# Merging two pairs of small matmul groups in a single-core diffusion step, with the instruction order set anew

## The chip, the core and the metric

The kernel runs on one core of a Trainium2 chip. The metric is device time in microseconds (us) of one execution. The core has a matmul engine (PE, with its weight loads shown apart as PEld), a vector engine (DVE), a scalar engine (ACT), a general engine (POOL) and a queue engine (SP) that only issues DMAs. Each engine runs its own instructions strictly in the order in which the program holds them, and waits at an instruction until what it needs is there.

## The reference

The reference computes one layer for 1024 latent tokens and 128 context tokens, with d_model 1024. Two token mixers read the same normalised, modulated input, through one projection:

```
u = h @ w_in                                   # 1024 -> 2560 (HGRN2) + 1760 (RWKV-7)
# HGRN2, 4 heads x 128, forward and backward, f = lb + (1 - lb) * sigmoid(z):
S = exp(b_last) * S + (k * exp(b_last - b))^T v ;  o = q * exp(b) S + (causal scores) v
# RWKV-7, 8 heads x 64, forward and backward, per token:
S = S * w - (S kk) (kk * a)^T + v k^T ;  y = S r
x = x + gate1 * (concat(o_a, o_b) @ w_out)
h = rmsnorm(x) * (1 + scale2) + shift2
x = x + gate2 * ((gelu(dwconv(h @ w_gate) + b) * (h @ w_up)) @ w_down)   # d_ff 2816
```

The outputs are the normalised tokens and the states that the context leaves in both mixers.

## The kernel before, in words

The whole step is recorded by a planner (class `Plan`) and then issued engine by engine. A recorded operation is one instruction, or a group made by `plan.together()`, which stands on its engine without anything between. The planner takes, for each engine in turn, the ready operation of the highest rank. The rank is the estimated rest of the path behind it, plus a lead by kind (`LEADS`) and a correction for each sixteen operations (`NUDGE`), less penalties for PE when the array's shape changes (`INTO`, `OUT`, `SWITCH`). Copies can go to ACT or DVE, and stores to POOL or SP, whichever the planner finds first. The order that results is fixed in the program.

Four stages follow one another, with overlap. They are named here by the lines of the profile.

- **Projections and RWKV features, about 60 to 500 us.** Lines L1125 to L1127 are the dense fp32r matmuls of the projection, three for each 128 rows of the contraction (high times high, low times high, high times low). Between them stand small fp32 groups of the RWKV features: `features(p, ...)` runs for 4 pairs of heads, over 3 blocks of 384 tokens each. In each block and each direction d it builds `kr` (L1452) and `kb` (L1453) on DVE, multiplies them chunk by chunk on PE in tiles of 64 x 32 (L1461 and L1462, 24 matmuls to a group, each run as two passes) into the PSUM tile `pk`, and copies the result out (L1469, L1475, L1477). `pk` has one buffer of two banks. `elim` (L1526, L1528) solves the small triangular systems.
- **Scans, about 500 to 1050 us.** `chains` is the sequential RWKV scan, 18 steps for each of two groups of heads (L1776, L1790, L1820, L1827, L1835, L1846). `hgrn_block(h, tb)` runs 12 times: it builds the HGRN2 scores in levels. Level 0 (L1631, 24 matmuls, tiles of 128 x 32) takes `kx` and `q2`; levels 1 to 5 (L1646) take `xs`, a copy of `kx` with the directions interleaved (L1643), and `qy` (L1618), which DVE updates between levels; `copy_predicated` (L1647) puts each level's part into `s32`. Then come L1652, L1658 and the transposes L1686 and L1691. The rest of the projection fills PE between these steps, and later the output projection (L2011 to L2013) with the row tiles' second norm and modulation (L2019, transposes L2025, L1991).
- **FFN up, about 1050 to 1535 us.** L2120, dense, with DVE's depthwise convolution (L2209) beside it. Its second half of tokens needs the quarter sums (L2057, L2053) of the row tiles that come last.
- **FFN down, to the end.** L2269 to L2271, dense. `finish` closes a row tile (L2290 to L2297), and `finish_last` the last one in pieces of 512, 256 and 256 columns (L2307 to L2323).

## Time and profile before

| what | us |
|---|---|
| median of 3 runs | 1820.85 (1820.06 to 1825.13) |
| the profiled execution | 1820.69 |
| its span, first to last instruction | 1818.9 |
| PE busy | 1768.3 (97%) |
| PE weight loads busy | 1587.1 (87%) |
| DVE busy | 1415.1 (78%) |
| ACT busy | 862.0 (47%) |

The granted TensorE clock was 0.993 over the span. Matmuls overlap in the pipeline and their ends are modelled, so a busy PE isn't one at its peak; what a matmul costs is read from the distance between the starts of neighbours.

### The profile page before, as it was taken

The numbers are of one execution on the slowest core, as the hardware profiler recorded it, in microseconds if no ns is written. First come the engines' busy times: TensorE is split into PE (matmuls) and PEld (weight loads), VectorE is DVE, ScalarE is ACT, GpSimd is POOL, SyncE is SP. The second block draws the span as 40 slices with busy tenths as digits, with TensorE's granted clock in tenths as the row PEclk, the third lists the DMA queues.
The fourth block names the chain that finished last, engine by engine and source line by source line (L and its number), as shares of the span: only waits on it lengthen the run. The fifth ranks groups of instructions, "written<-read, shape, count | busy, mean of one in ns | idle before, by whom it ended". The sixth has DMA issues, their size and how long they took to land.

```text
span 1818.9 us, 45180 instructions
## 1 busy us (share of the span) xinstructions
PE 1768.3 (97%) x18402; PEld 1587.1 (87%) x18402; DVE 1415.1 (78%) x2670; ACT 862.0 (47%) x1753; POOL 289.3 (16%) x553
## 2 busy tenths in 40 slices
PE   7999999999999999999999999999999999999998
PEld 5889888899888788888788799999999999888887
DVE  7559899887778888876867889999999954985543
ACT  6556656543255645643636754444444433321321
POOL 2013435353312222122110100000000000000000
PEclk9999999999999999999999999999999999999999
DMA  9325637487757568889967522222222247774451
GB/s 325 102 72 151 147 102 180 128 229 193 207 165 246 165 203 258 267 283 306 324 207 244 203 59 73 73 73 73 73 73 73 76 126 251 227 272 162 133 169 67
DMA packets 272176, 307.45 MB, mean 169 GB/s; under 512 B 62611, under 2 KB 216849, under 8 KB 271968
## 3 DMA queue, kind: packets, MB, share of 16 engines
q1 hardware_dynamic: 245584, 224.33, 41.3%
q0 software_dynamic: 26384, 80.23, 13.1%
q8 instruction: 144, 2.36, 0.5%
q14 instruction: 64, 0.52, 0.1%
HBM read 200.50 MB, written 103.99 MB: 167 GB/s over the span
## 4 chain that ended last, share of the span: by engine, by line
PE 69%; DMA 5%; DVE 3%; ACT 1%; issue 1%; POOL 0%; SPq 0%; DVEq 0%; ACTq 0%; POOLq 0%
PE banks L2120 27%; PE banks L2269 5%; PE banks L2270 5%; PE banks L2271 5%; PE banks L1125 3%; PE banks L1127 3%; PE banks L1126 3%; DMA low<-d_ak 2%; PE banks L2011 2%; PE banks L2013 2%; PE banks L2012 2%; PE banks L1776 1%; PE banks L1827 1%; PE banks L1846 1%; PE banks L1646 1%
## 5 line engine op out<-in xcount | busy, mean ns | idle before, releaser
L1125 PE MATMUL banks<-hh,wh 128*128 128x384 f32 x768 | 282.0, 367 | 0.7 <-DVE fx L1314 0.7
L1127 PE MATMUL banks<-hh,wl 128*128 128x384 f32 x768 | 259.0, 337 | 0.0
L1126 PE MATMUL banks<-hl,wh 128*128 128x384 f32 x768 | 258.7, 337 | 0.0
L2209 DVE SCALAR_TENSOR_TENSOR low<-low,pf 128x1024 f32<-128x1024 f32 x176 | 224.8, 1279 | 4.6 <-ACT low L2203 3.0
L2120 PE MATMUL banks<-qm,wh 128*128 128x320 f32 x968 | 223.3, 310 | 0.0
L2120 PE MATMUL banks<-hbm,wh 128*128 128x256 f32 x880 | 164.4, 283 | 1.3 <-ACT low L1991 1.3
L1125 PEld LDWEIGHTS banks<-hh,wh 128*128 128x128 f32 x768 | 144.9, 189 | 21.0 <-issue 11.4
L2120 PE MATMUL banks<-qm,wl 128*128 128x320 f32 x528 | 162.8, 308 | 0.0
L2120 PEld LDWEIGHTS banks<-qm,wh 128*128 128x128 f32 x968 | 160.7, 189 | 0.1
L1126 PEld LDWEIGHTS banks<-hl,wh 128*128 128x128 f32 x768 | 145.5, 189 | 2.4 <-issue 1.2
L1127 PEld LDWEIGHTS banks<-hh,wl 128*128 128x128 f32 x768 | 145.0, 189 | 0.0
L2120 PEld LDWEIGHTS banks<-hbm,wh 128*128 128x128 f32 x880 | 140.4, 191 | 1.7 <-ACT low L1991 1.7
L2120 PE MATMUL banks<-ham,wh 128*128 128x256 f32 (+1 forms) x616 | 132.4, 295 | 0.0
L2120 PE MATMUL banks<-hbm,wl 128*128 128x256 f32 x440 | 124.8, 284 | 0.0
L2120 PEld LDWEIGHTS banks<-ham,wh 128*128 128x128 f32 x616 | 102.2, 192 | 0.0
L2120 PEld LDWEIGHTS banks<-qm,wl 128*128 128x128 f32 x528 | 99.1, 188 | 0.0
L2269 PE MATMUL banks<-qm,hbm 128*128 128x512 f32 (+1 forms) x240 | 93.7, 390 | 0.0
L2270 PE MATMUL banks<-qm,hbm 128*128 128x512 f32 (+1 forms) x240 | 93.6, 390 | 0.0
L2271 PE MATMUL banks<-qm,hbm 128*128 128x512 f32 (+1 forms) x240 | 93.5, 390 | 0.0
L2090 ACT CAST wh<-fx 128x512 fp32r<-128x512 f32 x88 | 54.3, 620 | 80.6 <-PE banks L2120 76.0
L2158 ACT COPY fx<-banks 128x320 f32<-128x320 f32 (+1 forms) x132 | 52.0, 397 | 84.2 <-PE banks L2120 82.8
L2120 PEld LDWEIGHTS banks<-hbm,wl 128*128 128x128 f32 x440 | 84.4, 192 | 0.0
(527 smaller groups left out, 4333.5 us busy)
## 6 DMA issues: line engine op xcount, KB each, us to landing
wr<-in_w_in_dram SPq DMA_DIRECT2D x34, 512.0 KB, 5.6
d_a<-low POOLq DMA_DIRECT2D x22, 576.0 KB, 3.4
low<-d_ak SPq DMA_DIRECT2D x64, 192.0 KB, 4.4
low<-in_ffn_w_up_dram SPq DMA_DIRECT2D x22, 512.0 KB
wr<-in_ffn_w_gate_dram SPq DMA_DIRECT2D x22, 512.0 KB, 3.7
low<-d_kb SPq DMA_DIRECT2D x36, 256.0 KB, 5.3
low<-d_a SPq DMA_DIRECT2D x12, 704.0 KB, 4.6
low<-in_ada_w_dram SPq DMA_DIRECT2D x32, 256.0 KB, 6.0
```

The costliest lines, as they stand in the source:

```text
L1125: mm(o, wh[:, kt, :], hh[:, kt, c], kt == 0, False)
L1126: mm(o, wh[:, kt, :], hl[:, kt, c], False, False)
L1127: mm(o, wl[:, kt, :], hh[:, kt, c], False, kt == KT - 1)
L2011: mm(ps, oh[:, kt, :], woh, kt == 0, False)
L2012: mm(ps, oh[:, kt, :], wol, False, False)
L2090: split(*w, src)
L2120: pe.matmul(o, a[:, kt, :], b[:, kt, :], start=start and first, stop=last, skip_group_check=not start)
L2158: act.copy(keep[n], y[:, 0:w])
L2209: dve.scalar_tensor_tensor(av, shifted(dy, dx), tap(3 * dy + dx), av, MUL, ADD)
L2269: mm(o, lh, w[:, 0, c], first, False)
L2270: mm(o, lh, w[:, 1, c], False, False)
L2271: mm(o, ll, w[:, 0, c], False, last)
```

## The change

It does three things. In `features` both directions of a block are prepared first, and then their 48 matmuls stand in one group, into one `pk` tile in which the directions lie 192 columns apart; the copies of both follow. In `hgrn_block` the copy `xs` for level 1 is made before level 0, and the matmuls of levels 0 and 1 (24 and 12) stand in one group, in two parts of one bank. And the planner's constants are new: `LEADS`, `NUDGE` and some single numbers, so that the order changes on every engine. The matmuls are the same in number and shape; lines of the changed program lie up to 14 higher behind the edits.

```diff
-LEAD_LAST = -10.47
-LEAD_ADA = -9.0
+LEAD_LAST = 42.88
+LEAD_ADA = -22.15
...
-INTO = 2.76
-OUT = 0.86
+INTO = 2.83
+OUT = 1.76
...
-HUNGRY = 2.04
-BUSY = 168.59
+HUNGRY = 0.4
+BUSY = 181.8
...
+            kept = []
             for d in range(2):
...
-                pk = view(tl("pk", [P, 1024]), 0, [[512, 2], [64, 3], [1, 64]])
-                with plan.together():
+                kept.append((kr, kb, dd, tw, src))
+            both = tl("pk", [P, 1024])
+            pks = [view(both, 192 * d, [[512, 2], [64, 3], [1, 64]]) for d in range(2)]
+            with plan.together():
+                for d in range(2):
+                    kr, kb, pk = *kept[d][:2], pks[d]
                     for ci in range(6):
                         for h in range(2):
                             hs = slice(64 * h, 64 * h + 64)
                             o = 64 * (ci % 2)
                             mm(pk[o:o + 32, h, ci // 2, :], kb[hs, ci, 64:96], kr[hs, ci, 0:64], True, True)
                             mm(pk[o + 32:o + 64, h, ci // 2, 0:32], kb[hs, ci, 96:128], kr[hs, ci, 32:64], True, True)
+            for d in range(2):
+                kr, kb, dd, tw, src = kept[d]
...
-        pv = part(0, 32)
+        p0, pv = part(0, 32), part(96, 32)
+        xs = tl("xs", [P, B])
+        copy(xs.rearrange("p (a b c) -> p a b c", b=2, c=1), view(kx, 0, [[2, B // 2], [B + 1, 2], [1, 1]]))
         with plan.together(s32, sc):
             for i in range(3):
                 for d in range(2):
                     for _, b, t0, r in quarters[4 * i:4 * i + 4]:
-                        mm(pv[r, i, :], kx[:, d, t0:t0 + 32], q2[:, t0:t0 + 32], d == 0, d == 1)
-        act.activation(s32, pv, AF.Copy, scale=0.5)
+                        mm(p0[r, i, :], kx[:, d, t0:t0 + 32], q2[:, t0:t0 + 32], d == 0, d == 1)
+            for i, b, t0, r in quarters:
+                mm(pv[r, i, :], xs[:, t0:t0 + 32], view(qy, t0, [[2, 16], [B + 1, 2]]), True, True)
+        act.activation(s32, p0, AF.Copy, scale=0.5)
...
-            if l < 6:
+            if l == 1:
+                dve.copy_predicated(s32, view(lmask, 0, [[0, 3], [1, 32]]), pv)
+            elif l < 6:
```

The first place where the order moves is ACT in the first features block (about 130 to 136 us before). L1469 and L1475 (L1477 and L1483 in the changed program) copy `pk` out, one pair of rows for each direction; L1440 (L1441) is the next block's first step. Before:

```order
L1469 COPY low<-banks 128x2x3x32
L1475 COPY top<-banks 32x2x96
L1341 COPY low<-banks 128x256
L1342 COPY low<-banks 128x128
L1440 ACTIVATE top<-banks,dp 128x6x64 x2
L1442 ACTIVATE top<-top,eps 128x6x64
L1469 COPY low<-banks 128x2x3x32
```

And in the changed program:

```order
L1341 COPY low<-banks 128x256
L1342 COPY low<-banks 128x128
L1477 COPY low<-banks 128x2x3x32
L1483 COPY top<-banks 32x2x96
L1477 COPY low<-banks 128x2x3x32
L1483 COPY top<-banks 32x2x96
L1441 ACTIVATE top<-banks,dp 128x6x64 x2
```

The copies of the second direction moved from behind the next block's first steps to directly behind those of the first direction.

The second place is ACT where the FFN begins (about 1036 to 1047 us before). L1134 and L1136 belong to a row tile's norm, L2019 (L2033) scales the row tile by it, which the transposes on PE wait for, L1991 (L2005) modulates what PE transposed, and L2053 (L2067) rounds a quarter for the FFN. Two row tiles pass here. Before:

```order
L2019 ACTIVATE low<-low 128x1024
L2158 COPY fx<-banks 128x320
L1136 ACTIVATE low<-low 128x1
L2053 CAST hbm<-fx 128x4x128
L1991 ACTIVATE low<-banks,modc,modA 128x128 x2
L2053 CAST hbm<-fx 128x4x128
L1991 ACTIVATE low<-banks,modc,modA 128x128 x3
L2019 ACTIVATE low<-low 128x1024
```

And in the changed program:

```order
L1136 ACTIVATE low<-low 128x1
L2067 CAST hbm<-fx 128x4x128 x2
L2033 ACTIVATE low<-low 128x1024
L2172 COPY fx<-banks 128x320
L2067 CAST hbm<-fx 128x4x128
L2067 CAST ham<-low 128x4x128
L2067 CAST hbm<-low 128x4x128
L2005 ACTIVATE low<-banks,modc,modA 128x128 x4
```

The second tile's L2033 now stands ahead of all modulation, and the first tile's modulation stands behind it, a copy and three roundings.

The third place is PE at the end of the program. L2269 to L2271 (L2283 to L2285) are the down projection; rows of 128x256 belong to `finish_last`, rows of 128x512 to its first piece or to the plain row tiles. Before, the program's last rows:

```order
L2269 MATMUL banks<-hbm 128x256
L2270 MATMUL banks<-hbm 128x256
L2271 MATMUL banks<-hbm 128x256
L2269 MATMUL banks<-qm,hbm 128x256
L2270 MATMUL banks<-qm,hbm 128x256
L2271 MATMUL banks<-qm,hbm 128x256
```

And in the changed program:

```order
L2283 MATMUL banks<-hbm 128x256
L2284 MATMUL banks<-hbm 128x256
L2285 MATMUL banks<-hbm 128x256
L2283 MATMUL banks<-qm,hbm 128x512
L2284 MATMUL banks<-qm,hbm 128x512
L2285 MATMUL banks<-qm,hbm 128x512
```

The last nine matmuls of a plain row tile's second half now stand behind the whole of `finish_last`. On DVE their evacuation and norm (L2304 to L2310) stand behind the last 256 columns of `finish_last`, and the products with the final norm's weight (L2326, twice), which stood between the pieces before (L2312), stand behind those:

```order
L2331 RECIPROCAL low<-low 128x1
L2304 TENSOR_TENSOR banks<-banks,fx 128x512
L2305 TENSOR_TENSOR fx<-banks,fx 128x512
L2307 TENSOR_TENSOR low<-low 128x1
L2309 RECIPROCAL low<-low 128x1
L2310 SCALAR_TENSOR_TENSOR fx<-fx,low 128x1024
L2326 TENSOR_TENSOR fx<-fx,low 128x512
L2326 TENSOR_TENSOR fx<-fx,low 128x256
L2334 SCALAR_TENSOR_TENSOR fx<-fx,low 128x256
L2335 TENSOR_SCALAR fx<-fx,low 128x256
```

That piece of DVE's order is the program's end; before, L2312 stood directly behind each L2308.

More of the change, by code (lines that the diff above doesn't have):

```diff
@@ L45 @@
 AHEAD = 240.0
-HUNGRY = 2.04
-BUSY = 168.59
-NUDGE = {1: 6, 3: -7, 4: -41, 5: -2, 7: 9, 8: 9, 9: 9, 10: 9, 11: 20, 12: 19, 13: 19, 14: 15, 15: 15, 16: 5, 17: -4, 18: -1, 19: -4, 20: -18, 21: -29, 22: -19, 23: -26, 24: -26, 25: -6, 27: -3, 28: -3, 29: -3, 30: -3, 31: -5, 32: -3, 33: -3, 35: -3, 51: -5, 52: -5, 53: -2, 84: -6, 85: -6, 86: -6, 87: -6, 88: 6, 91: -3, 92: -6, 93: -6, 94: -6, 95: -6, 96: -6, 97: -6, 98: -6, 104: -7, 105: -4, 108: -6, 109: 4, 110: -6, 111: -6, 119: 6, 127: -7, 140: 6, 141: 6, 142: 6, 143: 21, 144: 6, 145: 6, 147: -2, 172: -17, 173: -17, 174: -17, 175: -17, 183: -14, 184: -20, 185: -4, 189: 57, 190: 57, 191: 69, 193: 5, 194: 3, 200: -15, 201: -8, 203: 11, 204: 14, 206: 3, 212: -16, 217: 13, 218: 5, 224: -48, 225: -15, 226: -15, 227: -15, 236: 7, 239: -2, 243: -26, 244: -26, 245: -26, 246: -19, 247: -26, 251: 7, 252: 7, 253: 5, 254: -12, 266: -4, 269: 3, 275: 61, 282: -16, 290: -9, 292: 2, 294: 18, 295: 18, 296: 18, 297: 28, 298: 28, 299: 28, 300: 48, 301: 48, 302: 30, 303: 27, 305: 30, 306: 30, 307: 30, 308: 37, 309: 40, 310: 40, 311: 40, 312: 51, 313: 42, 314: 47, 315: 43, 316: 23, 317: 26, 318: 26, 319: 23, 320: 23, 321: 23, 322: 23, 323: 22, 328: 10, 329: 13, 330: 29, 331: 29, 337: -10, 338: -10, 339: -10, 340: -10, 341: -10, 342: -10, 343: -10, 344: 10, 345: 10, 346: 5, 347: 8, 348: 8, 349: 8, 350: 11, 351: 8, 352: -12, 353: -14, 354: -8, 355: -14, 356: 15, 357: -2, 358: 33, 359: 7, 360: -4, 361: 4, 362: -3, 363: -4, 364: 7, 365: -7, 367: 13, 368: 23, 370: 25, 377: 6, 378: 13, 379: 13, 380: 18, 381: 18, 382: 18, 390: 1, 396: 6, 398: 5, 400: -10, 401: -10, 404: -6, 405: -6, 406: -6, 407: -6, 408: -6, 409: -6, 410: -6, 411: -6, 412: -6, 413: -2, 416: -23, 417: 3, 418: 3, 419: 3, 425: -3, 426: -3, 427: -3, 428: -3, 453: -3, 454: -3, 455: -5, 456: 20, 457: 5, 458: 20, 459: 3, 460: -15, 461: 1, 462: -4, 463: -11, 464: -4, 465: -4, 466: -4, 467: -4, 468: -4, 469: -2, 470: 32, 471: 15, 472: 15, 473: 16, 474: 1, 475: 1, 476: 15, 477: 10, 478: 14, 479: 15, 480: 28, 481: 10, 482: 12, 483: 34, 484: 24, 485: 26, 486: 6, 487: 21, 488: 6, 489: 11, 490: 20, 491: 13, 492: 25, 493: 2, 494: -16, 495: -5, 496: -5, 497: -5, 498: -5, 499: -43, 500: -20, 501: -18, 502: -16, 503: -39, 504: -13, 505: -12, 506: -12, 507: -15, 508: -36, 509: -37, 510: -24, 511: -24, 512: -38, 516: 21, 517: 22, 518: 22, 519: 11, 520: 11, 521: 11, 522: 1, 523: 11, 524: 1, 525: 11, 526: 9, 527: 26, 528: -1, 529: 1, 530: -5, 532: -34, 533: -34, 534: -26, 535: -27, 536: 8, 537: 22, 538: 22, 539: 45, 540: 16, 541: 18, 542: 14, 543: 14, 544: 4, 545: 13, 546: 4, 547: 4, 548: 53, 549: 39, 550: 39, 551: 52}
@@ L49 @@
-LEADS = {'ada_block': 46.4, 'bonus_rows': 27.8, 'chains': -35.7, 'const': 113.0, 'conv_rkv': 0.0, 'down_weights': -36.2, 'elim': -4.6, 'features': 0.0, 'ffn_down': 14.5, 'ffn_mid': -1.7, 'finish': 52.5, 'finish_last': -12.3, 'first_columns': -38.6, 'front': 0.0, 'gate_row': 0.0, 'hgrn_block': -3.6, 'hgrn_in': 0.0, 'hgrn_out': 113.5, 'late': -0.7, 'made': 3.5, 'mod_columns': -1.2, 'mod_scale': 70.4, 'modulated': -24.2, 'pair': 8.2, 'param_loads': 9.6, 'params': -96.8, 'post': 3.0, 'prep': 119.5, 'product': -3.4, 'put': 0.0, 'save': 4.8, 'step_kernel': -1.0, 'stored': 0.0, 'three': -10.1, 'total': -0.3, 'turned': 4.0, 'weights': 0.0, 'wo_tile': 5.1}
+HUNGRY = 0.4
@@ new lines @@
+BUSY = 181.8
+NUDGE = {1: 6, 3: -7, 4: -84, 5: -80, 6: -51, 7: -57, 8: -42, 9: -42, 10: -42, 11: -31, 12: -22, 13: -32, 14: 15, 15: 15, 17: -11, 18: -1, 19: -4, 21: -29, 22: -19, 23: -56, 24: -66, 25: 9, 26: 18, 27: 23, 28: 7, 29: 7, 30: 7, 32: -3, 34: 2, 35: -3, 41: -5, 50: -42, 51: -47, 52: -47, 53: -44, 54: -42, 55: -42, 56: -42, 58: 10, 59: -1, 62: 11, 63: 8, 64: 31, 65: 8, 66: 8, 67: 8, 68: 1, 69: 1, 70: -13, 71: 1, 72: 1, 73: 1, 74: 1, 75: 1, 76: 1, 77: 1, 78: 1, 79: 1, 80: 1, 81: -3, 82: 1, 83: 1, 84: -5, 85: -5, 86: 1, 87: -5, 88: 7, 89: 1, 90: 1, 91: -2, 92: -5, 93: -5, 94: -5, 95: -17, 96: -17, 97: -5, 98: -18, 99: -10, 100: -10, 101: -10, 102: -10, 103: -12, 104: -19, 105: -16, 106: -12, 107: -12, 108: -18, 109: -6, 110: -18, 111: -29, 112: -18, 113: -21, 114: -21, 115: -21, 116: -21, 117: -47, 118: -21, 119: -8, 120: -21, 121: -26, 122: -26, 123: -5, 124: -9, 125: -9, 126: -9, 127: -16, 128: -10, 129: -9, 130: -9, 131: -26, 132: -9, 133: -7, 134: 7, 135: 2, 137: 7, 138: 7, 139: 7, 140: 7, 141: -17, 142: 7, 143: 7, 145: 5, 146: 5, 147: -2, 148: -3, 149: -8, 150: -3, 151: -3, 152: -53, 153: -76, 154: -72, 155: -68, 156: -19, 157: 33, 159: 14, 168: 3, 171: 21, 178: -37, 183: 18, 184: -14, 186: -16, 187: 2, 188: 2, 189: 7, 190: -10, 191: 2, 192: 2, 193: -5, 194: -5, 195: -5, 196: 6, 198: -6, 199: -15, 200: -15, 201: -15, 202: -15, 203: -17, 204: -7, 209: 2, 218: 18, 219: -6, 223: 7, 227: 18, 228: 18, 229: 18, 230: 18, 231: 28, 232: 18, 233: 33, 234: 18, 236: -1, 240: 21, 241: 26, 242: 9, 243: -4, 244: -4, 245: -14, 247: 6, 248: 7, 252: -1, 253: -1, 254: -1, 255: -2, 259: 34, 270: 7, 273: -31, 274: -28, 275: -28, 276: -32, 278: -18, 282: -1, 283: -1, 295: 37, 296: 37, 297: 13, 300: 10, 301: -21, 302: 2, 303: 8, 304: 24, 305: 6, 306: 6, 307: 6, 308: 5, 311: 32, 314: -21, 315: 9, 316: 56, 317: 3, 318: 3, 319: 1, 320: -15, 321: 3, 322: -6, 324: 4, 327: -46, 328: -50, 329: -57, 330: -7, 331: -7, 332: -7, 333: -3, 335: -4, 336: -7, 337: -7, 338: -6, 339: -6, 340: -14, 341: -6, 342: -4, 343: -5, 344: -6, 347: -5, 348: -5, 349: -6, 350: -7, 351: -6, 352: 6, 353: -6, 354: -4, 355: -12, 356: -4, 357: 8, 358: -4, 359: -4, 360: -8, 361: -4, 362: 10, 363: -6, 364: -6, 365: -6, 366: 14, 367: 10, 368: 24, 370: 21, 371: 23, 372: 12, 373: 13, 374: 3, 375: 3, 376: 3, 377: 2, 378: 1, 379: 1, 380: 1, 381: -10, 382: -5, 383: -5, 384: 1, 385: -5, 386: 2, 387: -5, 388: -5, 389: -2, 390: 6, 391: 12, 392: 12, 393: 1, 394: -5, 396: -5, 397: -5, 398: -5, 400: -5, 401: -5, 402: -5, 403: 16, 404: 56, 405: 2, 406: -5, 407: -5, 408: -5, 409: -5, 410: 10, 411: 11, 412: -5, 413: 2, 415: -5, 416: 4, 418: -15, 419: -7, 422: 5, 424: 5, 425: 5, 426: -7, 428: -3, 434: 20, 435: -10, 436: -16, 439: -6, 440: -6, 441: 17, 442: 14, 443: 22, 445: 18, 446: -6, 447: -6, 448: -11, 449: -11, 450: -7, 451: -6, 452: -13, 453: -8, 454: 6, 455: 3, 456: -10, 458: 4, 459: -5, 460: -2, 461: -10, 462: 5, 463: -4, 464: -2, 465: -9, 466: -3, 467: -5, 468: -5, 469: -6, 470: -9, 471: 1, 472: -4, 473: 1, 474: -6, 475: 1, 476: -6, 477: -16, 478: -6, 479: -6, 480: -6, 481: -31, 483: -6, 484: -7, 485: 15, 486: -7, 487: -7, 488: -7, 489: 11, 490: 18, 491: 18, 492: 22, 493: 130, 494: 88, 495: 106, 496: 97, 497: 36, 498: 1, 499: 1, 500: 15, 501: 8, 502: 8, 503: -6, 504: -10, 505: -17, 506: -17, 507: -17, 508: -17, 509: -17, 510: -17, 511: -17, 512: -10, 513: -30, 514: -67, 515: -74, 516: -55, 517: -18, 518: -64, 519: -43, 520: -43, 521: -43, 522: -43, 523: -73, 524: -20, 525: -67, 526: -43, 527: -43, 528: -49, 529: -49, 530: -49, 531: -59, 532: -44, 533: -38, 534: -38, 538: -18, 539: -18, 540: -18, 541: -18, 542: -18, 543: -18, 544: -18, 545: -18, 546: -34, 547: -18, 548: -18, 549: -6, 553: -38, 554: -48, 555: -48, 556: -39, 558: -38, 559: -10, 560: -10, 561: -10, 562: 2}
@@ new lines @@
+LEADS = {'ada_block': 46.4, 'bonus_rows': 38.1, 'chains': -35.7, 'const': 79.7, 'conv_rkv': 0.0, 'down_weights': -38.3, 'elim': -4.6, 'features': 0.0, 'ffn_down': -16.6, 'ffn_mid': -1.7, 'finish': 52.5, 'finish_last': -12.3, 'first_columns': -38.6, 'front': 0.0, 'gate_row': 40.5, 'hgrn_block': -10.4, 'hgrn_in': -3.9, 'hgrn_out': 116.9, 'late': -0.7, 'made': 15.0, 'mod_columns': -1.2, 'mod_scale': 70.4, 'modulated': -32.6, 'pair': 8.2, 'param_loads': 42.8, 'params': -104.3, 'post': 3.0, 'prep': 119.5, 'product': -18.6, 'put': -3.5, 'save': -17.1, 'step_kernel': -1.0, 'stored': 44.5, 'three': -26.1, 'total': -5.1, 'turned': 39.7, 'weights': 0.0, 'wo_tile': 5.1}
@@ L1432, in features, with src @@
                 w, g = 2 * (p % 2) + d, p // 2
-                def src(a, lo):
+                def src(a, lo, d=d):
                     a = a[:, lo:lo + 384]
@@ L1462, in features @@
                             mm(pk[o + 32:o + 64, h, ci // 2, 0:32], kb[hs, ci, 96:128], kr[hs, ci, 32:64], True, True)
+            for d in range(2):
+                kr, kb, dd, tw, src = kept[d]
+                pk, sg, w, g = pks[d], tb if d == 0 else 2 - tb, 2 * (p % 2) + d, p // 2
+                c0 = 6 * sg
                 lat = (0, 2) if (d, sg) == (0, 2) else (1, 3) if (d, sg) == (1, 0) else (0, 3)
```

## The prediction

> **What bounds the kernel now.** I read the page first, then the table of stages, then PE's waits, and last the timeline at the places that the order moves.

> ```profile
> span 1818.9 us, 45180 instructions
> PE 1768.3 (97%) x18402; PEld 1587.1 (87%) x18402; DVE 1415.1 (78%) x2670; ACT 862.0 (47%) x1753; POOL 289.3 (16%) x553
> PE 69%; DMA 5%; DVE 3%; ACT 1%; issue 1%; POOL 0%; SPq 0%; DVEq 0%; ACTq 0%; POOLq 0%
> ```

> The span is 1818.9 us, and the profiled execution took 1820.69 us, so 1.8 us lie around the span. The median of the runs is 1820.85 us, 0.16 us above it. I make the sum against 1820.69. PE is busy for 97% and carries 69% of the chain that ended last; no other engine has more than 3% of that chain, and all DMA has 5%. The table of stages (PE, PEld, DVE, ACT, POOL, each with its count) shows where PE leaves anything:

> ```profile
> 0.00:100.00 100.00, 87.70 (x555) 72.73 (x556) 60.44 (x154) 57.57 (x118) 16.68 (x48) 0.98 0.62 197
> 100.00:500.00 400.00, 392.38 (x4400) 351.85 (x4398) 335.92 (x687) 212.60 (x421) 149.53 (x270) 1.00 0.60 159
> 500.00:1050.00 550.00, 526.06 (x8585) 451.33 (x8586) 433.18 (x1004) 305.59 (x691) 100.07 (x193) 0.99 0.75 238
> 1050.00:1500.00 450.00, 450.00 (x3370) 450.00 (x3370) 397.12 (x597) 196.03 (x383) 12.90 (x23) 0.99 0.25 78
> 1500.00:1819.00 319.00, 312.21 (x1498) 261.21 (x1496) 188.42 (x232) 90.19 (x145) 10.09 (x19) 0.99 0.55 182
> ```

> PE's idle time is 12.3 us in the first 100, where the changed order is nearly the old one, 7.6 in the features, 23.9 in the scans, none in the FFN's first half, and 6.8 at the end, nearly all of it behind the last matmul. A change that adds no PE work and takes none away can therefore move little: the loss at changes of tile shape, some of the 31.5 us of waits in the middle, the start of the FFN, and the tail.

> **What a visit to small tiles costs.** From the timeline of PE, one features group between dense matmuls, and a return from full-size fp32 transposes:

> ```profile
> 148.82 0.34 PE L1127 MATMUL banks<-hh,wl 128*128 128x384 f32 x1
> 149.09 0.24 PE L1461 MATMUL banks<-top 64*32 64x64 f32 x1
> ...
> 149.59 0.22 PE L1461 MATMUL banks<-top 64*32 64x64 f32 x1
> 149.73 0.44 PE L1125 MATMUL banks<-hh,wh 128*128 128x384 f32 x1
> 150.01 0.34 PE L1126 MATMUL banks<-hl,wh 128*128 128x384 f32 x1
> 150.19 0.35 PE L1127 MATMUL banks<-hh,wl 128*128 128x384 f32 x1
> 783.40 0.42 PE L1125 MATMUL banks<-hh,wh 128*128 128x384 f32 x1
> 783.65 0.34 PE L1126 MATMUL banks<-hl,wh 128*128 128x384 f32 x1
> 783.83 0.34 PE L1127 MATMUL banks<-hh,wl 128*128 128x384 f32 x1
> ```

> Dense starts lie 0.18 us apart (150.01 to 150.19). Into the group it takes 0.27 (0.09 more), from its last matmul to the next dense one 0.14 where neighbours within the group lie some 0.01 apart (0.13 more), and the first dense interval is 0.28 (0.10 more). A visit costs about 0.33 us beside its matmuls. The features' groups fall from 24 to 12, so a merge that only does that saves 12 x 0.33 = 4.0 us. In the scans levels 0 and 1 stood side by side already in 5 of the 12 blocks; the other 7 save 7 x 0.33 = 2.3 us.

> The new order spends part of that. I counted all changes between dense, full-size fp32 and each smaller tile shape in both programs' PE order: up to the first L1776 they fall from 240 to 221, from there to the FFN they rise from 486 to 492, and behind that they stay at 4. Priced by kind with the median distances of this trace (a full-size fp32 group is nearly free to enter, but its return costs 0.25 - 0.18 = 0.07, as at 783.40), the features save 2.6 us and the scans 0.2. I take **-2.8 us**; the bounds are 0, should other waits lie under these gaps, and -6.3, both merges in full.

> [...]

> **The waits that the merges remove or add.** The list of PE's waits (total, times, longest):

> ```profile
> PE banks L1461 <- DVE low L1477: 1.3, 2, 0.8
> PE banks L1461 <- DVE top L1452: 0.4, 1, 0.4
> PE banks L1461 <- DVE top L1475: 0.3, 1, 0.3
> PE banks L1646 <- DVE top L1618: 1.2, 2, 0.8
> PE banks L1631 <- ACT top L1617: 1.2, 2, 0.9
> PE banks L1776 <- DMA low<-d_ak: 2.5, 6, 1.0
> ```

> L1477 and L1475 are the copies out of `pk`: the second direction's group waited until the first had left the one buffer. With both in one tile that wait inside a block is gone, 1.6 us; the next block's group comes a block later and finds the tile empty. The wait for L1452 (the operand `kr`) stays. The merged group can be late because it needs both directions' `kr` and `kb`; what is queued behind it is the dense work, and for it wait the copies and the next `elim`. The order puts 6 to 30 dense matmuls (1 to 5 us) ahead of most merged groups, so I take nothing for that, with 12 x 0.8 us (the longest of these rows) as the other end. In the scans, the merged group waits for `xs` and `qy` where level 0 alone waited for `kx` (L1617), and level 1 then for `qy` (L1618): the later of the two remains, so I take 0, between -1.2 and +12 x 0.8. Together **-1.6 us**. ACT and DVE keep their counts within 12 instructions, so no term stands for them.

> **The start of the FFN.** PE, DVE and ACT rows of the timeline:

> ```profile
> 1033.57 0.39 PE L2013 MATMUL banks<-wom,wl 128*128 128x512 f32 x1
> 1039.94 0.15 DVE L1137 RECIPROCAL low<-low 128x1 f32<-128x1 f32 x1
> 1040.01 0.67 DVE L2053 TENSOR_TENSOR ham<-fx,ham 128x512 fp32r<-128x512 f32 x1
> 1042.01 0.41 DVE L1991 TENSOR_SCALAR low<-banks,modA,modc 128x128 f32<-128x128 f32 x1 [1.33 <-ACT low L1991]
> 1045.62 1.97 PE L2025 MATMUL banks<-c_ident,low 128*128 128x128 f32 x8 [3.75 <-DVE fx L2057]
> 1048.90 0.80 PE L2120 MATMUL banks<-hbm,wh 128*128 128x256 f32 x2 [1.31 <-ACT low L1991]
> ```

> The last output projection ends at 1033.96 (1033.57 + 0.39), and dense work runs without a break from 1048.90, 14.9 us later. Before and after, 48 dense matmuls and 16 transposes stand between. The wait of 3.75 us is for L2019 of the second tile, which ACT held behind five modulations; the change puts it ahead of them, so that wait shrinks. But the modulations come later. From the last L2015 to the second tile's L1137 DVE had 8 products and roundings, in 6.0 us (1039.94 - 1033.96); by the order it has 11, and three more of 0.67 us, which overlap by a little, are 1.7 us. Before the first modulation it then has six more (4.0 us), where before the modulation came 2.1 us after L1137 (1042.01 - 1039.94), 1.9 us more. That is 1.7 + 1.9 = 3.6 us later; the shorter wait of the second transposes, whose banks come free earlier, gives some 1.6 of it back. I take **+2.0 us**, between 0 and +3.6.

> **The tail.** The last pieces of `finish_last`, and a plain row tile's end just before:

> ```profile
> 1796.76 0.70 DVE L2290 TENSOR_TENSOR banks<-banks,fx 128x512 f32<-128x512 f32 x1 [6.23 <-PE banks L2271]
> 1799.75 1.28 DVE L2296 SCALAR_TENSOR_TENSOR fx<-fx,low 128x1024 f32<-128x1024 f32 x1
> 1805.87 0.69 DVE L2312 TENSOR_TENSOR fx<-fx,low 128x512 f32<-128x512 f32 x1
> 1809.25 0.42 DVE L2312 TENSOR_TENSOR fx<-fx,low 128x256 f32<-128x256 f32 x1
> 1811.93 0.28 PE L2271 MATMUL banks<-qm,hbm 128*128 128x256 f32 x1
> 1812.25 0.43 DVE L2307 TENSOR_TENSOR banks<-banks,fx 128x256 f32<-128x256 f32 x1 [2.11 <-PE banks L2271]
> 1814.30 0.48 DVE L2320 SCALAR_TENSOR_TENSOR fx<-fx,low 128x256 f32<-128x256 f32 x1
> 1814.70 0.35 DVE L2321 TENSOR_SCALAR fx<-fx,low 128x256 f32<-128x256 f32 x1
> 1815.51 0.38 SPq L2322 DMA_DIRECT2D out_y_sample_dram<-fx  x1
> ```

> Now DVE starts 0.04 us after the last matmul and is done 2.80 us later (1812.25 to 1815.05); the outputs' DMAs take 3.85 more to the span's end. In the changed program the last matmuls are a plain tile's, so DVE goes from L2290 to the end of L2296, 4.27 us (1796.76 to 1801.03), and then through L2312 twice, L2320 and L2321: 0.69 + 0.42 + 0.48 + 0.35 = 1.94. That is 6.2 instead of 2.8 us. One of the two DMAs is issued earlier meanwhile, which saves its 0.4. I take **+3.0 us**, between +1.5 (the plain tile's chain alone) and +3.4.

> **The sum**: -2.8 - 1.6 + 2.0 + 3.0 = +0.6, that is 1820.69 + 0.6 = 1821.3 us. The other 700 us of mixed work get a new order whose waits I can't read from rows; I give them 0, with 5 us either way from the 31.5 us of idle PE there.

> **The rivals.** *The merges pay in full.* Then the shape changes bring 6.3 us, `pk` 1.6, the waits for `d_ak` (2.5 us) go because 1776 stands farther from the last use of its operands, and the FFN's start costs nothing; with the tail's 3.0 it gives 1820.69 - 6.3 - 1.6 - 2.5 + 3.0 = 1813.3. For it: the chain of waits is PE's, so every gap counts. Against it: the scans' count of shape changes rises. *The merged groups wait.* Each needs the slower of two chains on DVE, which is 84% busy from 100 to 500 us (335.92 of 400). If DVE is late by 0.8 us, as the longest rows are, at 12 of the 24 merged groups, that costs 9.6 us over the forecast: 1830.9. It decides from about 6 such groups on (4.8 us). For it: waits for DVE end before these very groups now. Against it: the dense work that is ordered ahead. *The order hides it all*, tail and FFN apart: if the gaps fill with other waits, nothing comes back and the time is 1820.69 + 5.0 = 1825.7; that lies inside the forecast's range.

> **How the numbers follow.** A measurement of this kernel can tell about 0.3% (5.5 us) from no change. The forecast, with the hiding case, has 0.52; the merges in full 0.18; the waiting groups 0.30. Faster by over 0.3% means below 1815.4, slower above 1826.3. From these cases: faster 0.18, same 0.52, slower 0.30. The forecast's own range is its 5 us either way, 1816 to 1826. The range for 8 in 10 reaches to both rivals: 1813 to 1831.

> **What the profile would show.** L1461 with half as many first-of-group gaps and no wait for L1477 or L1475; L1631 and the first L1646 without a gap; at the FFN's start L2025 twice without 3.75 us between, but L2120's restart some 17 us behind the last L2013; and 9 to 10 us from the last matmul to the span's end instead of 6.7. Wrong would be a tail as short as now, DVE waits in front of L1461 of several us in total, or a PE idle time between 100 and 1050 us that differs from 31.5 by more than 5.

## The result, and the profile after

The changed program is slower: 1837.01 us (1836.52 to 1840.48, 4 runs) beside 1820.45 us for the one before (1820.05 to 1825.13, 4 runs), a ratio of 1.0089 [1.0068, 1.0110]. Measured again later, beside other runs of the old one, it gave 1.0075 [1.0053, 1.0097]. The forecast was 1821.3 us, with 1813 to 1831 as the range for 8 in 10. The loss is 14 to 17 us, and the measured time lies above that range.

The page of the changed program (span; busy time and count of each engine; shares of the chain that ended last):

```profile
span 1838.7 us, 45180 instructions
PE 1768.7 (96%) x18402; PEld 1586.2 (86%) x18402; DVE 1414.2 (77%) x2658; ACT 862.9 (47%) x1763; POOL 304.7 (17%) x571
PE 85%; DMA 7%; DVE 5%; ACT 2%; issue 2%; SPq 1%; POOL 0%; DVEq 0%; ACTq 0%; POOLq 0%
```

PE is busy for 1768.7 us where it was 1768.3: the work is the same, and the time has gone into idle PE. By stage (length, then PE, PEld, DVE, ACT and POOL, each with its count, the granted clock, DMA):

```profile
0.00:100.00 100.00, 86.83 (x556) 71.48 (x556) 61.94 (x156) 56.01 (x115) 17.88 (x50) 1.00 0.63 202
100.00:500.00 400.00, 392.06 (x4445) 353.61 (x4444) 333.73 (x684) 217.73 (x438) 158.45 (x280) 1.00 0.60 160
500.00:1050.00 550.00, 519.83 (x8500) 443.26 (x8496) 420.65 (x966) 293.10 (x665) 105.34 (x200) 0.99 0.76 235
1050.00:1500.00 450.00, 443.77 (x3305) 442.23 (x3306) 401.43 (x608) 201.32 (x394) 12.37 (x22) 0.99 0.23 75
1500.00:1839.00 339.00, 326.20 (x1606) 275.65 (x1604) 196.40 (x246) 94.74 (x155) 10.63 (x20) 0.98 0.53 177
```

Idle PE is 30.2 us in the scans' row where it was 23.9, 6.2 in the row from 1050 us where it was 0, and 12.8 at the end where it was 6.8. The features' row hardly changes (7.9 and 7.6), although 45 more matmuls lie in it. The FFN's start lay before 1050 us and now lies across it, so the rows blur the scans: between the first L1776 (L1790) and the last L2013 (L2027) alone, PE's idle time is 31.7 us where it was 20.1. The list of PE's waits (total, times, longest) shows what is new:

```profile
PE banks L1849 <- issue: 4.1, 2, 3.1
PE banks L1790 <- DMA low<-d_ak: 4.1, 7, 1.5
PE banks L1660 <- issue: 2.8, 2, 2.1
PE banks L1467 <- issue: 2.2, 1, 2.2
PE banks L1841 <- issue: 1.9, 1, 1.9
PE banks L2134 <- ACT hbm L2067: 1.8, 1, 1.8
PE banks L2134 <- ACT wh L2104: 1.6, 1, 1.6
PE banks L2134 <- DVE hbm L2067: 0.9, 1, 0.9
```

"issue" means that PE waited for nothing that the profile shows: the wait has no releaser, that is, nothing is seen to end it. The old program's list has only these two larger ones of that kind:

```profile
PE banks L1827 <- issue: 1.4, 2, 1.0
PE banks L1776 <- issue: 0.8, 1, 0.8
```

Over the whole list "issue" rises from 2.2 to 12.6 us, waits for DMA from 3.7 to 7.6, for ACT from 8.9 to 12.0, and those for DVE fall from 27.6 to 24.0. These are one execution each, and only "issue" stands out: `before_shift`, a near copy of the old program that comes further down, has 10.8 us of waits for DMA and 1.8 of "issue". One "issue" wait on PE's timeline, in the middle of a group of 32 matmuls whose operands all came from earlier steps, and the two ends of what follows it:

```profile
650.82 0.29 PE L1851 MATMUL banks<-low,c_ident 128*64 128x64 f32 x4
650.94 0.22 PE L1849 MATMUL banks<-low 128*64 128x64 f32 x1
654.26 0.27 PE L1849 MATMUL banks<-low 128*64 128x64 f32 x2 [3.11 <-issue]
654.32 0.23 PE L1851 MATMUL banks<-low,c_ident 128*64 128x64 f32 x1
...
655.13 0.52 PE L1126 MATMUL banks<-hl,wh 128*128 128x384 f32 x1
655.45 0.52 PE L1127 MATMUL banks<-hh,wl 128*128 128x384 f32 x1
...
658.72 0.34 PE L1126 MATMUL banks<-hl,wh 128*128 128x384 f32 x1
658.90 0.34 PE L1127 MATMUL banks<-hh,wl 128*128 128x384 f32 x1
```

PE stops for 3.3 us, and the dense matmuls just behind start 0.32 us apart, where 3 us later they are at 0.18 again. The table by stretch (same columns; the clock is the last but two) shows why:

```profile
647.00:650.40 3.40, 3.25 (x108) 2.87 (x110) 2.12 (x7) 1.98 (x7) 1.81 (x4) 1.00 0.96 279
650.94:654.26 3.32, 0.22 (x7) 0.14 (x4) 1.44 (x6) 0.24 (x2) 0.00 (x0) 1.00 0.51 160
654.64:658.06 3.42, 3.42 (x25) 2.76 (x24) 0.89 (x3) 0.00 (x0) 0.00 (x0) 0.51 0.22 52
```

The granted clock halves (0.51) for 3.4 us right behind the stop. So this stop costs its own length and, by an estimate from the row (half of 3.4 us), up to 1.7 us more, and those 1.7 us don't show as idle time. Not every stop is followed by half clock (last section).

### The profile page after: what moved, and what is told of

Its sections match the earlier page's. It is cut to its first block, busy times and chain, and to the rows that moved or that the text cites. A ratio compares the mean times of both kernels' runs of the same rounds, so it can differ in the third digit from the quotient of the medians.

```text
span 1838.7 us, 45180 instructions
## 1 busy us (share of the span) xinstructions
PE 1768.7 (96%) x18402; PEld 1586.2 (86%) x18402; DVE 1414.2 (77%) x2658; ACT 862.9 (47%) x1763; POOL 304.7 (17%) x571
## 3 DMA queue, kind: packets, MB, share of 16 engines
q8 instruction: 144, 2.36, 0.5%
## 4 chain that ended last, share of the span: by engine, by line
PE 85%; DMA 7%; DVE 5%; ACT 2%; issue 2%; SPq 1%; POOL 0%; DVEq 0%; ACTq 0%; POOLq 0%
PE banks L2134 26%; PE banks L1125 7%; PE banks L1126 6%; PE banks L1127 6%; PE banks L2283 5%; PE banks L2284 5%; PE banks L2285 5%; PE banks L1790 2%; PE banks L2025 2%; PE banks L2027 1%; PE banks L2026 1%; DMA low<-d_ak 1%; DMA top<-d_hu 1%; PE banks L1363 1%; PE banks L1841 1%
## 5 line engine op out<-in xcount | busy, mean ns | idle before, releaser
L1125 PE MATMUL banks<-hh,wh 128*128 128x384 f32 x768 | 282.5, 368 | 2.9 <-DVE fx L1314 1.5
L1127 PE MATMUL banks<-hh,wl 128*128 128x384 f32 x768 | 258.8, 337 | 0.0
L1126 PE MATMUL banks<-hl,wh 128*128 128x384 f32 x768 | 258.7, 337 | 0.0
L2134 PE MATMUL banks<-qm,wh 128*128 128x320 f32 x968 | 224.1, 311 | 1.6 <-ACT wh L2104 1.6
L2134 PE MATMUL banks<-hbm,wh 128*128 128x256 f32 x880 | 164.4, 283 | 2.7 <-ACT hbm L2067 1.8
L1125 PEld LDWEIGHTS banks<-hh,wh 128*128 128x128 f32 x768 | 145.0, 189 | 24.3 <-issue 13.3
L2134 PE MATMUL banks<-qm,wl 128*128 128x320 f32 x528 | 163.3, 309 | 0.7 <-DVE wl L2104 0.7
L2134 PEld LDWEIGHTS banks<-qm,wh 128*128 128x128 f32 x968 | 161.3, 189 | 2.0 <-ACT wh L2104 1.9
L1126 PEld LDWEIGHTS banks<-hl,wh 128*128 128x128 f32 x768 | 145.4, 189 | 2.3 <-issue 1.2
L1127 PEld LDWEIGHTS banks<-hh,wl 128*128 128x128 f32 x768 | 144.9, 189 | 0.0
L2134 PEld LDWEIGHTS banks<-hbm,wh 128*128 128x128 f32 x880 | 139.9, 190 | 3.1 <-ACT hbm L2067 2.0
L2134 PE MATMUL banks<-ham,wh 128*128 128x256 f32 (+1 forms) x616 | 132.1, 295 | 0.0
L2134 PE MATMUL banks<-hbm,wl 128*128 128x256 f32 x440 | 124.7, 283 | 0.0
L2134 PEld LDWEIGHTS banks<-ham,wh 128*128 128x128 f32 x616 | 101.9, 191 | 0.0
L2134 PEld LDWEIGHTS banks<-qm,wl 128*128 128x128 f32 x528 | 99.4, 188 | 0.9 <-DVE wl L2104 0.9
L2233 POOL DMA_DIRECT2D d_a<-low x22 | 11.7, 532 | 459.9 <-DVE low L2232 184.4
L2104 ACT CAST wh<-fx 128x512 fp32r<-128x512 f32 x88 | 53.9, 619 | 71.9 <-PE banks L2134 62.9
L2283 PE MATMUL banks<-qm,hbm 128*128 128x512 f32 (+1 forms) x221 | 86.4, 391 | 0.0
L2284 PE MATMUL banks<-qm,hbm 128*128 128x512 f32 (+1 forms) x221 | 86.4, 391 | 0.0
L2285 PE MATMUL banks<-qm,hbm 128*128 128x512 f32 (+1 forms) x221 | 86.3, 390 | 0.0
```

The costliest lines, as they stand in the source:

```text
L1125: mm(o, wh[:, kt, :], hh[:, kt, c], kt == 0, False)
L1126: mm(o, wh[:, kt, :], hl[:, kt, c], False, False)
L1127: mm(o, wl[:, kt, :], hh[:, kt, c], False, kt == KT - 1)
L2104: split(*w, src)
L2134: pe.matmul(o, a[:, kt, :], b[:, kt, :], start=start and first, stop=last, skip_group_check=not start)
L2283: mm(o, lh, w[:, 0, c], first, False)
```

## What the stops are

I counted PE's instructions in each trace (a matmul and its weight load are two; a small fp32 matmul runs as two passes, 1152 records of L1461 and L1462 in `before` for 24 groups of 24 matmuls, and so is four; the instructions in which PE waits for a semaphore count too). In the 14 profiles of this study PE has 96 "issue" waits of 0.3 us or more behind the first 100 us, and 94 of them stand at one place: at the instruction with number 256 k + 193. The other two end at groups whose operands come by DMA. The page's queue table has the fetches:

```profile
q8 instruction: 144, 2.36, 0.5%
```

144 packets carry 2.36 MB, and 36,804 matmuls and weight loads over 144 are 256 instructions to a packet of 16 KB. So PE gets its program in blocks of 256 instructions, 128 passes, and where it comes to a border before the next block is there, it stops. The times of q8's packets in the traces show this directly. At all 94 stops PE goes on 1.1 to 1.8 us after the end of the packet that holds the next block, and at none of the other 1920 borders behind the first 100 us does a block start less than 1.2 us after its packet's end. For each profile I summed the time over 0.1 us at these borders, from 100 to 1050 us: 3.7 us in the old program, 14.9 in the changed one.

The theory for the experiments ("supply") is that the new order and the larger groups pack small matmuls more densely in time, so that PE runs out of instructions more often. The rivals: the merged groups cost by their data; the waits without a releaser are for data that the profile doesn't show; the stops cost nothing, since PE would wait there anyhow.

## The experiments

**By place.** In four kernels the planner's rank is replaced by a given order, so that the old and the new order can be joined at a stage's border:

```diff
-                r = op.tail + op.lead
+                return -float(RANK[op.id])
```

Given the old program's order, such a kernel is that program row for row, and likewise for the changed one. `s1_features` has the new order and the merged groups up to the end of the features, and the old order behind.

> The changed program's order and merged groups up to the end of the features (the 12 merged groups of 48), and from there the old order to the last instruction, with levels 0 and 1 apart. Theory 'places' (the features gain what was forecast; the new order loses in the scans and at the end): 1820.4 - 3.0 = 1817.4 us, since the first L1776 came at 479.4 us in the changed program and at 482.4 before. Rival 'merges' (the large groups themselves cost, by the waits and bursts that they bring): no gain or a loss, 1820 to 1826.

Measured: 1820.9 us, ratio 0.9993 [0.9975, 1.0010].

> The changed program's order up to the end of the scans (about 1000 us), then the old order of the FFN and its end. 'Places': the scans' loss is all in it and the tail's 6 us are not; 1817.4 + 11.6 = 1829 us, and the list of PE's waits holds some 10 us of waits without a releaser inside groups. Rival 'merges': the same waits, but m_levels has them too. A rival of the end ('the FFN's order and the tail carry most of it'): 1822 or less.

Measured: 1830.67 us, ratio 1.0041 [1.0025, 1.0058].

> The changed program's order up to the middle of the down projection, then the old order of the last rows. 'Places': 1837.0 - 5.9 = 1831.1 us, 2 us over s2_scans, which is what the FFN's start costs; from the last matmul to the end of the span 7 us instead of 12.9. If the tail's lateness is only what the earlier loss pushes along, it stays at 1837.

Measured: 1832.41 us, ratio 1.0053 [1.0034, 1.0071].

> As s1_features, and with levels 0 and 1 merged in the scans, in which the order is the old one as far as the merged groups allow. 'Places' (order, not merging, costs in the scans): within 3 us of s1_features, 1815 to 1820. 'Merges': 1825 or more, with waits inside or ahead of the groups of 36.

Measured: 1825.51 us, ratio 1.0014 [1.0001, 1.0027].

The old program ran at 1823.1 us beside these, 2.7 over the 1820.4 from which the expectations were worked out, so the ratios count. Their steps are -1.3 us for the features, which can't be told from 0, +8.8 for the scans, +2.2 for the FFN, and the rest to 1.0075 or 1.0089, 4 to 6.6, for the last rows. The scans, the FFN and the tail are where "places" put the loss, with less in the scans than the 11.6 us that it named. `s1_features` doesn't decide between "places" and "merges": its interval holds a gain of 3 us as well as none. `m_levels` fits neither cleanly: 1825.51 us is a time that "merges" named, but beside the old program it is only 2.6 us more [0.2, 4.9], and it is 3.9 us over `s1_features`, with intervals that overlap. The traces give the same places. Positions of PE's marks (us), from the first L1776 to the last projection (L2013), to the first down matmul (L2269), to the last matmul and to the end:

| kernel | first L1776 | scans | FFN up | FFN down | tail |
|---|---|---|---|---|---|
| before | 482.4 | 551.2 | 502.9 | 275.4 | 7.0 |
| s1_features | 479.7 | 558.1 | 502.7 | 275.4 | 7.0 |
| s2_scans | 477.5 | 566.8 | 502.2 | 275.4 | 7.2 |
| s3_ffn | 479.1 | 562.9 | 505.6 | 275.0 | 7.2 |
| after | 479.4 | 566.6 | 505.0 | 274.8 | 12.9 |
| after_again | 477.9 | 566.3 | 505.1 | 274.9 | 12.9 |

FFN and tail repeat within half a microsecond. The scans of one program differ by 7 us between executions (551.2 and 558.1 have the same order), so their 9 us are read from the runs and not from one trace.

**Are the merged levels to blame?** `levels_apart` is `s2_scans` with levels 0 and 1 in groups of their own:

```diff
-            for i, b, t0, r in quarters:
-                mm(pv[r, i, :], xs[:, t0:t0 + 32], view(qy, t0, [[2, 16], [B + 1, 2]]), True, True)
```

(that line goes back behind level 0's evacuation).

> As s2_scans (new order to the end of the scans, old order after it), but with levels 0 and 1 in groups of their own as before, level 1 where it stood in the old program's sequence as far as the new order allows. If the order and not the merging of the levels costs the scans their 9 us: as s2_scans, ratio 1.003 to 1.006, 1828 to 1831. If the merged levels cost it: 1.000, 1820 to 1823.

Measured: 1834.06 us, ratio 1.0065 [1.0040, 1.0089], above the range that I gave, and not faster than with the merged levels. So in the new order it isn't the merged group that costs the scans their 9 us, but the order.

**The supply by itself.** `bench` adds work of no use behind the old program's end:

```diff
+        def small():
+            with plan.together():
+                for ci in range(12):
+                    for h in range(2):
+                        hs, o = slice(64 * h, 64 * h + 64), 64 * (ci % 2)
+                        mm(both[o:o + 32, h, 0:64], ident[hs, 32:64], ident[hs, 0:64], True, True)
+                        mm(both[o + 32:o + 64, h, 64:96], ident[hs, 96:128], ident[hs, 32:64], True, True)
...
+        for count, gap in ((24, 0), (12, 12), (12, 24)):
+            dense(64)
+            for _ in range(count):
+                small()
+                if gap:
+                    dense(gap)
```

> The kernel before, with work of no use behind its end: 64 dense matmuls, 24 groups of 48 small matmuls (tiles of 64x32, as L1461) back to back, 64 dense, 12 such groups with 12 dense between, 64 dense, 12 groups with 24 dense between. All operands are there and nothing else runs. Theory 'supply' (PE gets its instructions in blocks of 256, which is 128 passes with their weight loads, and stops where the next isn't there yet): the first 300 to 450 passes at 0.01 us, then a stop of 2 to 4 us every 128 passes, so the 2304 passes take 70 to 110 us instead of 24; with 12 dense (2.6 us) between, 96 passes in 3.6 us are still too fast and stops remain; with 24 dense (5.2 us) few or none. Rival 'operands' (the stops without a releaser are waits for data that the profile doesn't show): no stops, 24 us.

Its first two stretches and its wait, from the table by stretch and the list of waits:

```profile
1828.90:1892.40 63.50, 35.02 (x2305) 31.08 (x2304) 0.00 (x0) 0.00 (x0) 0.00 (x0) 0.55 0.02 4
1909.00:1954.30 45.30, 45.30 (x1285) 35.99 (x1284) 0.00 (x0) 0.00 (x0) 0.00 (x0) 1.00 0.01 3
...
PE banks L2333 <- issue: 28.5, 17, 2.0
```

Back to back, 2304 passes take 63.5 us instead of 24: the first border, 74 passes in, runs through, and at the other 17 PE stops for 1.7 to 2.3 us, each time at 256 k + 193, 3.7 us apart. The stops are 28.5 us of it; in the rest the clock stays near half (0.55). That is less than the 70 to 110 us that I expected, and the stops begin earlier, after 202 passes. With 12 dense between, 96 passes and 12 dense in 4.0 us, there is no stop at all, and none with 24. So "operands" falls, and my expectation that stops remain there was wrong: with no other traffic the supply held at 27 passes per us, and where PE stopped at each border it delivered 34 (128 in 3.7 us). In the features and scans, with DMA at 60 to 76%, stops come behind blocks that took up to 7.4 us, 17 passes per us (`before_shift`, block 52, a stop of 1.1 us).

**Do the stops go with the borders?** `after_shift` runs 32 matmuls of the first merged group twice, so that all later instructions stand 128 places on; `before_shift` does the same to the old program.

```diff
                 e, l = op.forms[0]
+                l = l + l[-24:] + l[-8:] if op.id == 649 else l
```

> The changed program in its own order, with 32 of the 48 small matmuls of the first merged group (133 us) run twice: 0.7 us of PE, and all later instructions of PE stand 128 places (64 passes) further on. In the profiles so far every stop inside a group without a releaser stands at a PE instruction number of 256 k + 193, and in the changed order at passes 3662, 5571, 7974, 9873 again and again. 'Supply': the stops stand at 256 k + 193 again, that is at other matmuls, and the old places run through; their sum may go either way, so 1837 with 6 us either way. 'Operands': the stops stay at the same matmuls, 1838.

Measured: 1837.87 us, ratio 1.0069 [1.0052, 1.0085].

> The old program in its own order, with the first L1461 group's matmuls repeated by the same 32. 'Supply', and the old order happens to have its bursts clear of the borders: its 3.7 us of stops at the borders become 8 to 12, and the time rises by 5 to 8 us to 1826 to 1829. If the borders don't matter to it: 1820 to 1823.

Measured: 1825.12 us, ratio 1.0006 [0.9990, 1.0021].

> The changed program's code and order unchanged, for its time beside the others and a second profile: 1837 us, ratio 1.009; the stops at the same passes 3662, 7974, 9873 with other lengths, if the borders set the place and the traffic the length.

Measured: 1838.76 us, ratio 1.0075.

From the lists of waits of `after_shift` (lines one higher):

```profile
PE banks L1661 <- issue: 3.6, 2, 1.9
PE banks L1667 <- issue: 1.9, 1, 1.9
PE banks L1863 <- issue: 1.8, 1, 1.8
```

In `after` and `after_again` blocks 28, 43, 51, 62 and 77 end in a stop (2.4 and 2.3 us for block 28, 3.3 and 0.6 for block 62). In `after_shift` none of these does; blocks 15, 48, 52, 68, 75, 79 and 80 stop instead, at 256 k + 193 again. The border sets the place. The length goes with the time at which the block's packet is issued: 0.8 to 1.7 us behind the border before at the 17 stops of `bench`, 1.1 to 6.1 us at the others. That the other traffic makes it late is likely, but no run shows it. And the sum hardly moves: 14.9 and 11.3 us before the shift, 14.4 with it; 3.7 us for the old program and 5.2 shifted. I had expected 8 to 12 there: that the old order merely has lucky borders isn't borne out at this shift, the only one that I ran. It is less dense: 13 blocks of the old program between 100 and 1050 us took under 5 us (without the stop at their end), and 21 of the changed one.

**Do the stops cost time?** In `pk_twice` every L1461 group of the old program runs its 24 matmuls twice: bursts of 96 passes, as in the merged groups, with the old data.

```diff
+                l = l + l if e == "PE" and l[0][3] == 1462 else l
```

> The old program in its own order, with every L1461 group's 24 matmuls run twice in place: bursts of 96 passes, as long as the merged groups, but with the old waits and the old number of visits. The direct price is 24 x 48 passes x 0.0105 us = 12.1 us. 'Supply, and the stops cost time': some of these bursts run into a border before the next instructions are there, 3 to 6 stops of 1 to 3 us and half-clock windows behind the longer ones; 12.1 + 6 to 12, ratio 1.010 to 1.013, with stops at 256 k + 193 inside L1461 groups. Rival 'a burst of this size is harmless': 12.1 us, ratio 1.0066.

Measured: 1843.32 us, ratio 1.0105 [1.0086, 1.0123], 19 us for 12.1 us of matmuls. The excess is 7 us [4, 10]. The trace has it in the features: the first L1776 comes 18.5 us later, of which 12.0 are passes and changes, and the borders' sum there goes from 0.1 to 7.5 us. The list of waits:

```profile
PE banks L1462 <- issue: 4.2, 5, 1.8
```

So a group of 96 small passes that stands where one of 48 stood is not harmless, and its stops are paid in full there.

`after_rot` tries the reverse in the changed program, with 39 dense triples drawn forward in the fixed order; `s1_rot` does it to three groups of `s1_features`:

```diff
-        self.order = sorted(ops, key=lambda o: (o.start, o.id))
+        self.order = [ops[i] for i in PLACES]
```

> The changed program in its order, with two to four groups of three dense matmuls (1.1 to 2.2 us) drawn forward from later dense runs to stand ahead of six of the places where PE stopped at a border (passes 2640, 2768, 5571, 6582, 9619, 9873); the number of changes between dense and small stays at 491, and nothing is added. 'Supply, and the stops cost time': the six places lose some 5 of the 6 to 7 us that they stopped, the sum at the borders falls from 11 to 15 us to 7 or 9, and the time by 4 to 6 us to 1832 (ratio 1.004 to 1.006). Rival 'the stops cover other waits': the borders' sum falls and the time stays at 1837, with new waits for DVE or DMA behind these places.

Measured: 1837.89 us, ratio 1.0099 [1.0070, 1.0127].

> As s1_features (new features, old scans and FFN), with two to five groups of three dense matmuls drawn forward ahead of three merged feature groups (passes 2768, 2896, 3790). 'Supply': the stop at 3790 (3.0 us in s1_features) and the smaller ones go, 1 to 3 us under s1_features: ratio to before 0.998 to 0.999, 1818. Rival: no change against s1_features.

Measured: 1823.66 us, ratio 1.0015 [0.9997, 1.0034].

In `after_rot` the borders' sum falls to 9.6 us, and four of the six places run through; but block 28 stops for 3.3 us (2.4 in `after`), block 22 anew, PE's waits for DMA are 9.6 us (7.6), and the time doesn't fall. That is what the rival "the stops cover other waits" named. In `s1_rot` the stop at 3790 goes and the time doesn't fall either. Both miss what "supply" named. Perhaps the dense work that is moved forward is then lacking elsewhere; no run shows that. No version beat the old program by more than can be measured; `s1_features` comes nearest.

## Why the prediction was wrong, step by step

- **The shape changes** (-2.8, bounds 0 and -6.3): right in kind, small by 1 to 4 us. Add up the shortest distances for each kind of neighbours, taken over all profiles: from 100 us to the first L1776 the sum falls by 2.7 to 4.7 us (I had 2.6), and in the scans by 0.6 to 2.2 (I had 0.2), by how finely the kinds are told apart. In `bench` a visit costs 0.11 us more into the group, 0.13 out of it and 0.13 at the first dense interval, 0.37 in all where I had 0.33. The traces give 3.8 to 6.9 us in all.
- **The waits for `pk`** (-1.6): right. L1467 has no wait for DVE or ACT any more; the list has it only with "issue". The merged groups don't wait for the slower direction either: the rival at 1830.9 had its sign and not its mechanism.
- **The start of the FFN** (+2.0): about right, 2.2 us by the runs and 2.1 to 3.4 by the table (505.0 to 505.6 against 502.2 to 502.9). The restart is 18.2 us behind the last L2013 (17 forecast, 14.9 before), and the wait of 3.75 us for L2019 is gone. From the timeline, the last projection and the two matmuls whose waits come last:

```profile
1045.99 0.39 PE L2027 MATMUL banks<-ham,wl 128*128 128x512 f32 x1
...
1063.32 0.36 PE L2134 MATMUL banks<-hbm,wh 128*128 128x256 f32 x1 [1.83 <-ACT hbm L2067]
1064.55 0.58 PE L2134 MATMUL banks<-hbm,wh 128*128 128x256 f32 x1 [0.88 <-DVE hbm L2067]
```

  In the place of the old wait stand three that the prediction hadn't named, the rows L2134 of the list above: the next weights' rounding on ACT (L2104), now behind the second tile's L2033, and the quarters' on ACT and DVE (L2067).
- **The tail** (+3.0, 9 to 10 us forecast): 12.5 us behind the last matmul instead of 6.7 (12.9 and 7.0 in the table, which counts from its start), so +5.8. DVE's rows:

```profile
1826.24 0.70 DVE L2304 TENSOR_TENSOR banks<-banks,fx 128x512 f32<-128x512 f32 x1
1829.17 1.29 DVE L2310 SCALAR_TENSOR_TENSOR fx<-fx,low 128x1024 f32<-128x1024 f32 x1
1833.19 1.03 DVE L2326 TENSOR_TENSOR fx<-fx,low 128x512 f32<-128x512 f32 x2 [2.73 <-DMA out_y_sample_dram<-fx]
1834.53 0.35 DVE L2335 TENSOR_SCALAR fx<-fx,low 128x256 f32<-128x256 f32 x1
```

  The chain is the one that I added up, but the term was too small by 2.8 us: L2326 also waits 2.73 us for a DMA, of which the sum had nothing: the last rows' `y` takes the buffer `f` that the plain row tile has just sent out, and there are two such buffers. 6.2 us were forecast and 8.7 came (1826.20 to 1834.88). With the old order of these rows (`s3_ffn`) the wait is gone and the tail is 7.2 us:

```profile
1824.76 0.16 DVE L2331 RECIPROCAL low<-low 128x1 f32<-128x1 f32 x1 [0.96 <-ACT low L2330]
1824.96 0.49 DVE L2334 SCALAR_TENSOR_TENSOR fx<-fx,low 128x256 f32<-128x256 f32 x1
```

- **The step that failed** is "The other 700 us of mixed work get a new order whose waits I can't read from rows; I give them 0, with 5 us either way". It was 12 us or so, and of one sign: features and scans together came out at +7.5 us by the runs, where the named terms gave -2.8 - 1.6 = -4.4. The sign that the prediction named for it is there: PE's idle time between 100 and 1050 us is 38.1 us, 6.6 more than 31.5 (34.7 in `after_again`). In the features the merged groups' stops give back much of what the changes save (borders there 0.1 to 0.4 us in profiles of the old program, 1.9 to 5.0 with the merged groups). In the scans, with the mean of six profiles of the new order against five of the old, 9.7 us are 5.1 at the borders, 3.2 in other waits of over 0.2 us, 2.3 in those of 0.05 to 0.2 us, and -0.9 elsewhere. The row in the old list that could have warned me is the "issue" wait of L1827: 1.0 us inside a group, put down to nothing. The 0.01 us between small matmuls, which I used for the price of a visit, is a rate that the supply didn't hold in `bench` (63.5 us for 2304 passes); the prediction priced a merge by its borders with dense work, and not by the density of instructions that it makes.

What stays open: the other 5 us of the scans. They are spread over many short waits for DMA, ACT and DVE, executions differ by more than that, and no run tells them apart. That the scans would get their border time back if the stops were removed was argued from `pk_twice`; `after_rot`, which tried it there, didn't show it, so how much of the scans' 9 us the stops cost is open too. The planner's weight for PE's instruction supply (`HUNGRY`) isn't the cause: with its old value the changed kernel gives the same program.

## What to carry to other kernels

When small matmuls are merged into longer groups, count instructions per microsecond as well as changes of shape: here a block of 256 PE instructions that ran in under some 5 us beside busy DMA risked a stop of up to 3.3 us (some stood behind slower blocks), and a saved visit brought only 0.33 to 0.37 us. A wait inside a group without a releaser in the profile is worth counting instructions to. At a program's end, follow the buffers as well as the engines: the last rows waited 2.73 us for a DMA whose tile they had to reuse.
